# One Silu at the end of the channel norm, and three of w_out's weight blocks moved ahead of the last modulation parts

## The chip, the cores and the metric

The kernel runs on one core of one Trainium2 chip. Its engines are TensorE (PE, matmuls; PEld is its weight load), VectorE (DVE), ScalarE (ACT), GpSimd (POOL) and SyncE (SP, which here only issues DMAs). Each engine executes its own queue in order, and semaphores make it wait for others. The metric is the device time of one execution in microseconds, as the median of several.

## The reference

The program is a chain of three parts on 272 tokens (16 meta tokens and 256 others) of width 1024: a first block of two layers, then a mixer and an expert layer with modulation. Only the first block is touched. One layer of it computes

```
hn = rmsnorm(h);  q, k, v, u = split(hn @ w_in)
attn = diff_attention(rope(q), rope(k), v)          # 4 heads, 128-query blocks, then an rmsnorm per head
z = a * sigmoid(gate);  z = causal depthwise conv(z, width 31) + conv_b
conv = silu(layer_norm(z) * ln_g + ln_b)            # over the 512 channels: the "channel norm"
h = h + concat([attn, conv]) @ w_out                # 512 + 512 channels in, 1024 out
h = h + (silu(gate) * up) @ w_down                  # gate, up from rmsnorm(h) @ w_gate_up
```

Beside that, a modulation row for the later parts is computed from a vector c: silu(c) @ w_ada + b_ada, 6144 wide, in 24 parts of 256 columns. Nothing in the first block needs it, so its parts are spread over the two layers as filler.

## The kernel before, in words

Activations lie transposed (channels on partitions, tokens along the row). Matmuls of large weights are done in three products of halves: a weight block of 1024 x 256 is loaded into a `raw` buffer (1 MB, one DMA of SP), ACT casts it to `hi` (line 165, two instructions of four k tiles each), DVE writes the rest raw - hi to `lo` (line 166, two instructions), and PE adds hi*xh (line 172), hi*xl (173) and lo*xh (174). There are three `raw`, three `hi` and three `lo` buffers; each is used in turn and waits until its last reader is done. `weights` (line 151) does the load and the conversion and raises its priority in the scheduler.

A modulation part (`ada_parts`, line 622) loads one block of w_ada into the same `raw` ring without converting it. PE runs eight narrow matmuls on it (line 628), ACT copies the row (631), PE sums it with two matmuls of one column (633), and DVE adds the bias (634).

The end of a layer's mixing is written as a string of steps, `ORDER` (line 32), one letter each: s scores, v values, a attention, c convolution, p modulation parts, n channel norm, w one w_out weight block. A scheduler with its own timeline orders the instructions of all engines from that and from priorities; the order it finds is fixed in the program. `ADA` (line 28) says how many modulation parts each layer takes.

Attention goes by query tiles (16, 128 and 128 tokens in layer 0, the last two in layer 1; here tile 1 and tile 2 are the two of 128). For a tile: transposes of the probabilities (451) and copies (453), the products with v (459), squares with sums on ACT (463), a square root on ACT and a reciprocal on DVE (201, 202), the scaled output `osb` on DVE (468), its transposes back on PE (472), and the write of the result into `cat`, the two halves of w_out's input, by ACT (475) and DVE (476). The names in the traces are those of buffers: `biga` holds the convolution's channels, `bigb` is `cat`.

The channel norm (line 501) sums the channels with matmuls of ones (505), subtracts the mean (508, 510), sums squares (512, 513), takes root and reciprocal of the variance (201, 202), and per 128 channels multiplies (517), then builds y * sigmoid(y) from Tanh: a Tanh (519) and an Identity (520) on ACT, their product on DVE (522), the halved high part into `cat` on ACT (524) and the rest on DVE (525).

The products with w_out (lines 562 to 572) take the heads' four k tiles first for the first five output blocks, so that they can start when the attention is done and the channel norm is not. Where ACT goes over to a function of another table (Sqrt, Tanh, Exp and Silu here), the program has an ACT_TABLE_LOAD ahead of it.

Of the kernel before, what the change touches and what calls it, by code (L numbers as in the profile page):

```python
# [9 lines left out]
F32 = mybir.dt.float32  # L10
F32R = mybir.dt.float32r
I32 = mybir.dt.int32
AF = mybir.ActivationFunctionType
OP = mybir.AluOpType

NM, S, D = 16, 256, 1024
T = NM + S
# [7 lines left out]
FIRST = 2000  # L25
LAM0 = [0.8 - 0.6 * math.exp(-0.3 * l) for l in range(2)]
EARLY = 1500
ADA = (12, 10, 2)
TAPS = (((0, 31), (1, 16)), ((0, 16),))
AHEAD = 5  # L30
PR0 = 9
ORDER = ("svacpnwwww", "svacpnwwww")


GQ, GK, GV, GZ, GB, DQ, DK, DV, GA, GBB = 0, 1024, 2048, 3072, 4096, 4112, 5648, 7184, 8720, 9744
# [74 lines left out]
class K:  # L110
# [195 lines left out]
    def first_block(s):  # L306
        nc, I, V, A, PE, SP, ap, cp = s.nc, s.I, s.V, s.A, s.PE, s.SP, s.ap, s.cp
# [3 lines left out]
        with s.tc.high_priority(offset=FIRST):  # L311
# [3 lines left out]
            P = s.columns(ap, ap, (("norm1_g", 16), ("b_glu", 16)), SP, tag="scr", bufs=3)  # L315
# [11 lines left out]
        for l in range(2):  # L327
            w_in = I["w_in"][l]
            tq = NM if l else 0
            nq = T - tq  # L330
# [9 lines left out]
            def sub(t, o, a):  # L340
                return t[:, o:o + a * T].rearrange("p (a b) -> p a b", a=a)
# [3 lines left out]
            acc = sub(s1, nz, 4)  # L345
            cat = (sub(s2, 0, KC), sub(s2, KC * T, KC))
# [3 lines left out]
            for b in range(2):  # L350
# [4 lines left out]
                for j in range(2):  # L355
                    c = 2 * b + j
# [30 lines left out]
            if l == 0:  # L387
                P.update(s.columns(ap, ap, (("norm2_g", 16), ("conv_b", 8), ("conv_ln_g", 8), ("conv_ln_b", 8),
                                            ("subln_g", 2)), s.G, tag="scr", bufs=3))
                subg = ap.tile([128, 2], F32, name="subg")  # L390
                hlg = ap.tile([128, 8], F32, name="hlg")
                hlb = ap.tile([128, 8], F32, name="hlb")
                for i in range(2):
                    V.tensor_scalar(subg[:, i:i + 1], P["subln_g"][:, i:i + 1], 1.0 - LAM0[i], None, op0=OP.mult)
                V.tensor_scalar(hlg, P["conv_ln_g"], 0.5, None, op0=OP.mult)
                V.tensor_scalar(hlb, P["conv_ln_b"], 0.5, None, op0=OP.mult)
                cw, nlam = s.first_params()
                s.ada()
            rcs, pro = [], []
# [79 lines left out]
            def conv():  # L479

                for c, n in TAPS[l]:
                    p = s.dx()
                    for j in range(n):
                        dg = ap.tile([128, 128], F32, name="dg", bufs=4)
                        A.activation(dg, ident, AF.Copy, scale=cw[:, l, 4 * j + c:4 * j + c + 1])
                        PE.matmul(p[:, :nq], dg, z[:, c, tq + j:tq + j + nq], start=(j == 0), stop=(j == n - 1))  # L486
                    A.activation(acc[:, c, :nq], p[:, :nq], AF.Identity, bias=P["conv_b"][:, 4 * l + c:4 * l + c + 1])
                tp = dict(TAPS[l])
                for c0 in (0, 2):
                    for j, c in [(j, c) for j in range(CW) for c in (c0, c0 + 1)]:  # L490
                        if j < tp.get(c, 0):
                            continue
                        zz = z[:, c, tq + j:tq + j + nq]
                        wj = cw[:, l, 4 * j + c:4 * j + c + 1]
                        if j == 0:
                            V.tensor_scalar(acc[:, c, :nq], zz, wj, P["conv_b"][:, 4 * l + c:4 * l + c + 1],
                                            op0=OP.mult, op1=OP.add)
                        else:
                            V.scalar_tensor_tensor(acc[:, c, :nq], zz, wj, acc[:, c, :nq], op0=OP.mult, op1=OP.add)

            def channel_norm():

                mu = s.ax()
                for c in range(4):
                    PE.matmul(mu[:, :nq], C["ones"], acc[:, c, :nq], start=(c == 0), stop=(c == 3))
                var = s.ax()
                sd = ap.tile([128, T], F32, name="sd")
                A.activation(sd[:, :nq], mu[:, :nq], AF.Copy, scale=1.0 / 512)
                for c in range(4):
                    V.tensor_tensor(acc[:, c, :nq], acc[:, c, :nq], sd[:, :nq], op=OP.subtract)  # L510
                    sq = ap.tile([128, T], F32, name="sq", bufs=3)
                    A.activation(sq[:, :nq], acc[:, c, :nq], AF.Square)
                    PE.matmul(var[:, :nq], C["ones"], sq[:, :nq], start=(c == 0), stop=(c == 3))
                s.rsqrt(sd[:, :nq], var[:, :nq], s.eps5, 1.0 / 512)
                for c in range(4):
                    i = 4 * l + c
                    V.tensor_tensor(acc[:, c, :nq], acc[:, c, :nq], sd[:, :nq], op=OP.mult)
                    th = ap.tile([128, T], F32, name="sq", bufs=3)
                    A.activation(th[:, :nq], acc[:, c, :nq], AF.Tanh, bias=hlb[:, i:i + 1], scale=hlg[:, i:i + 1])
                    A.activation(acc[:, c, :nq], acc[:, c, :nq], AF.Identity, bias=P["conv_ln_b"][:, i:i + 1],  # L520
                                 scale=P["conv_ln_g"][:, i:i + 1])
                    V.scalar_tensor_tensor(acc[:, c, :nq], th[:, :nq], 1.0, acc[:, c, :nq], op0=OP.add, op1=OP.mult)
                    ch = cat[0][:, 4 + c, tq:]
                    A.activation(ch, acc[:, c, :nq], AF.Copy, scale=0.5)
                    V.scalar_tensor_tensor(cat[1][:, 4 + c, tq:], acc[:, c, :nq], 0.5, ch.bitcast(F32), op0=OP.mult,
                                           op1=OP.subtract)


            v = s1[:, nz + 12 * T:nz + 12 * T + 1536].rearrange("p (a b) -> p a b", a=3)

            def values():

                for b in range(2):
                    w = s.weights(w_in, 0, 8, 1024 + 256 * b)
                    pvv = s.block2([(w, 8, 0)], x, 0, T)
                    vf = ap.tile([128, 2, T], F32, name="vf", bufs=2)
                    for j in range(2):
                        V.tensor_tensor(vf[:, j], pvv[j][:, :T], r, op=OP.mult)
                    for i, (t0, n) in enumerate(QT):
                        p = s.ax()  # L540
                        for j in range(2):
                            PE.transpose(p[:n, j * 128:(j + 1) * 128], vf[:, j, t0:t0 + n], ident)
                        A.copy(v[:n, i, 256 * b:256 * b + 256], p[:n, :256])


            wo = []
            for step in ORDER[l]:
                if step == "a":
                    attention()
                elif step == "s":  # L550
                    scores()
                elif step == "v":
                    values()
                elif step == "c":
                    conv()
                elif step == "n":
                    channel_norm()
                elif step == "w":
                    wo.append(s.weights(I["w_out"][l], 0, 8, 256 * len(wo)))
                else:  # L560
                    s.ada_parts(ADA[l])
            h1 = s.hp.tile([128, KC, T], F32, name="h", bufs=2)
            ps = [(s.mm, s.mm, s.mm, s.dx, s.dx, s.ax)[j]() for j in range(AHEAD)]
            for j in range(AHEAD):
# [29 lines left out]
            if l:  # L594
                s.mix_begin()
                wada = s.ada_ahead(ADA[2])
            for b in range(4):
                ws = [(s.weights(I["w_down"][l], k0 * 128, nk, 256 * b), nk, k0) for k0, nk in ((0, 8), (8, 8), (16, 6))]
                for j, p in enumerate(s.block2(ws, (fh, fl), tq, nq)):
                    V.tensor_tensor(h[:, 2 * b + j, tq:], p[:, :nq], h1[:, 2 * b + j, tq:], op=OP.add)  # L600
                    if l:
                        with s.tc.high_priority(offset=PRI):
                            s.mix_tile(h, h1, 2 * b + j)
        s.ada_parts(ADA[2], wada)
        s.h, s.hg = h, h1
# [1122 lines left out]
```

## Time and profile before

| | |
|---|---|
| median of 3 runs | 1663.44 us (1661.53 to 1663.89) |
| profiled execution | 1670.4 us, span 1668.6 us |
| mean granted clock of PE | 0.981 |
| busy in the span: PE, DVE, ACT | 1603.3, 862.3, 757.1 us |
| DMA, mean over the span | 233 GB/s |

Times in the trace are counted from the start of the span. A line of a timeline has start, length, engine, source line, operation, output and inputs, count, and in brackets the idle time ahead of it with what ended it. A long matmul is recorded in two pieces, so "x16" on line 628 is eight matmuls, and "x24" on line 459 is twelve. The clock in the tables of stages is the share of PE's full speed that was granted; 1.00 is 2.4 GHz and 0.50 is 1.2 GHz. The DMA share counts the time that packets took, against 16 engines, and can pass 1.

### The profile page before, as it was taken

Reading aid. Unit: us, or ns where it says so; the run is one execution under the profiler, and the core shown is the slowest. Engines: PE = TensorE matmul, PEld = TensorE weight load, DVE = VectorE, ACT = ScalarE, POOL = GpSimd, SP = SyncE. Lnnn points to the kernel's source line nnn. Section 1 sums busy time; section 2 is a strip of 40 time slices with the busy share of each in tenths; the row PEclk is TensorE's granted clock in tenths of the full one; section 3 lists DMA queues with packets and bytes.
Section 4 is the critical chain, followed back from the end, with each engine's and each line's share of the span. In section 5 each row is a group of like instructions: output and inputs, shape, how many; then the busy total and the mean of one; then the engine's idle time right before and its main releaser. Section 6 shows DMA issues by size and latency. Waiting matters only on the chain.

```text
span 1668.6 us, 32896 instructions
## 1 busy us (share of the span) xinstructions
PE 1603.3 (96%) x13616; PEld 1358.8 (81%) x13616; DVE 862.3 (52%) x1763; ACT 757.1 (45%) x1548; POOL 14.5 (1%) x28
## 2 busy tenths in 40 slices
PE   6998999999999999998999999999899999999997
PEld 6965999999967999988999899999666576556563
DVE  5685766646986666448655654554322221222122
ACT  5375644435437544455855866743322221222221
POOL 2000000000000000000000000000000000000000
PEclk9999999999988999999999999999999999999999
DMA  8408555555455555653333333556799999999995
GB/s 240 149 26 266 194 179 174 172 178 168 136 177 172 182 189 184 215 191 122 126 128 102 102 128 102 192 192 226 314 380 420 421 419 420 420 419 420 421 419 245
DMA packets 209958, 389.29 MB, mean 233 GB/s; under 512 B 8854, under 2 KB 183312, under 8 KB 184976
## 3 DMA queue, kind: packets, MB, share of 16 engines
q1 hardware_dynamic: 209104, 386.66, 63.1%
q8 instruction: 108, 1.77, 0.4%
q0 software_dynamic: 704, 0.51, 0.3%
q14 instruction: 42, 0.34, 0.1%
HBM read 386.10 MB, written 1.05 MB: 232 GB/s over the span
## 4 chain that ended last, share of the span: by engine, by line
PE 83%; DMA 7%; ACT 5%; DVE 3%; issue 1%; SPq 0%; ACTq 0%; DVEq 0%
PE mm L172 14%; PE mm L174 14%; PE mm L173 14%; PE pm L1542 9%; PE pm L1568 5%; DMA we<-in_w_exp_up 5%; PE pm L1505 3%; PE dx L486 2%; PE mm L195 1%; PE mm L196 1%; PE mm L197 1%; PE dx L628 1%; PE mm L459 1%; PE acc L1586 1%; ACT hi L165 1%; PE ax L274 1%
## 5 line engine op out<-in xcount | busy, mean ns | idle before, releaser
L166 DVE TENSOR_TENSOR lo<-raw,hi 128x1024 fp32r<-128x1024 f32 (+2 forms) x300 | 347.8, 1191 | 144.7 <-ACT hi L165 143.5
L165 ACT CAST hi<-raw 128x1024 fp32r<-128x1024 f32 (+2 forms) x300 | 292.7, 1024 | 267.6 <-PE mm L173 154.0
L172 PE MATMUL mm<-xh,hi 128*128 128x272 f32 (+1 forms) x1008 | 288.1, 288 | 0.0
L173 PE MATMUL mm<-xl,hi 128*128 128x272 f32 (+1 forms) x1008 | 287.8, 286 | 0.0
L174 PE MATMUL mm<-xh,lo 128*128 128x272 f32 (+1 forms) x1008 | 286.6, 286 | 0.0
L1542 PE MATMUL pm<-we,xT 128*32 128x256 f32 (+2 forms) x2048 | 194.2, 389 | 6.3 <-DMA we<-in_w_exp_up 5.5
L173 PEld LDWEIGHTS mm<-xl,hi 128*128 128x128 f32 x1008 | 189.7, 188 | 0.9
L174 PEld LDWEIGHTS mm<-xh,lo 128*128 128x128 f32 x1008 | 189.3, 188 | 0.5
L172 PEld LDWEIGHTS mm<-xh,hi 128*128 128x128 f32 x1008 | 188.5, 188 | 0.8
L1542 PEld LDWEIGHTS pm<-we,xT 128*32 128x32 f32 (+2 forms) x2048 | 123.1, 129 | 72.6 <-DMA we<-in_w_exp_up 7.8
L173 PE MATMUL mm<-bigb,hi 128*128 128x256 f32 (+1 forms) x512 | 148.6, 291 | 0.0
L172 PE MATMUL mm<-hh,hi 128*128 128x256 f32 x384 | 110.5, 291 | 7.3 <-ACT hh L702 4.2
L1568 PE MATMUL pm<-we,hT 128*32 128x512 f32 (+2 forms) x512 | 114.8, 599 | 0.4 <-DMA we<-in_w_exp_down 0.3
L173 PE MATMUL mm<-hl,hi 128*128 128x256 f32 x384 | 109.6, 286 | 0.7 <-DVE hl L703 0.7
L174 PE MATMUL mm<-hh,lo 128*128 128x256 f32 x384 | 108.6, 286 | 0.0
L1553 DVE SCALAR_TENSOR_TENSOR hp<-sil,cs,pm 128x256 f32<-128x256 f32 x26 | 17.6, 676 | 164.8 <-ACT sil L1551 164.8
L174 PE MATMUL mm<-biga,lo 128*128 128x272 f32 (+1 forms) x352 | 101.4, 288 | 0.0
L172 PE MATMUL mm<-biga,hi 128*128 128x272 f32 (+1 forms) x352 | 100.6, 286 | 0.0
L173 PEld LDWEIGHTS mm<-bigb,hi 128*128 128x128 f32 x512 | 97.9, 191 | 0.5
L1573 DVE TENSOR_TENSOR y<-pm,gt 128x512 f32<-128x512 f32 x52 | 35.8, 689 | 107.4 <-PE pm L1568 107.4
L195 PE MATMUL mm<-hi,hh 128*128 128x256 f32 x288 | 86.0, 299 | 2.0 <-DVE cacc L859 2.0
L1551 ACT ACTIVATE sil<-pm 128x256 f32<-128x256 f32 x26 | 10.0, 385 | 170.2 <-PE pm L1542 170.2
(544 smaller groups left out, 3102.7 us busy)
## 6 DMA issues: line engine op xcount, KB each, us to landing
we<-in_w_exp_gate SPq DMA_DIRECT2D x64, 1024.0 KB, 18.2
we<-in_w_exp_up SPq DMA_DIRECT2D x64, 1024.0 KB, 19.5
we<-in_w_exp_down SPq DMA_DIRECT2D x64, 1024.0 KB, 17.7
raw<-in_w_in SPq DMA_DIRECT2D x62, 1024.0 KB, 5.0
raw<-in_w_gate_up SPq DMA_DIRECT2D x44, 1024.0 KB, 5.0
raw<-in_w_ada SPq DMA_DIRECT2D x22, 1024.0 KB, 6.2
raw<-in_w_down SPq DMA_DIRECT2D x16, 1024.0 KB, 5.1
raw<-in_w_out SPq DMA_DIRECT2D x12, 1024.0 KB, 5.4
```

Of the source, the lines that this page charges most:

```text
L165: s.A.copy(hi[:, a:b], raw[:, a:b])
L166: s.V.tensor_tensor(lo[:, a:b], raw[:, a:b], hi[:, a:b].bitcast(F32), op=OP.subtract)
L172: s.PE.matmul(ps[:, :n], a, xh, start=start, stop=False)
L173: s.PE.matmul(ps[:, :n], a, xl, start=False, stop=False)
L174: s.PE.matmul(ps[:, :n], b, xh, start=False, stop=stop)
L195: s.PE.matmul(p[:, :256], xh, w[0][:, k], start=(k == 0), stop=False)
L486: PE.matmul(p[:, :nq], dg, z[:, c, tq + j:tq + j + nq], start=(j == 0), stop=(j == n - 1))
L1505: s.PE.matmul(p[:, 256 * kk:256 * kk + 256], s.ht[h][:, i, k + kk], oh[:, i], start=(i == 0 and h == 0), stop=(i == 1 and h == 1))
L1542: mm = PE.matmul(gu[sg, 256 * m:256 * m + 256], xT[:, k, o + sg.start:o + sg.stop], w[m][:, k], start=(k == 0), stop=(k == 7))
L1553: V.scalar_tensor_tensor(hp.rearrange("p k q -> p q k"), sil.rearrange("p (q k) -> p q k", k=2), cs, gu[:, 256:].rearrange("p (q k) -> p q ...
L1568: PE.matmul(py[sg], hT[:, k, sg], w[2][:, k, 512 * j:512 * j + 512], start=(k == 0), stop=(k == 1))
L1573: V.tensor_tensor(y, py, s.gt2[:, 512 * j:512 * j + 512], op=OP.mult)
```

## The change

Two edits. The channel norm's end is one Silu with scale and bias (ACT, in place), a cast to the high half and one subtraction; a Silu of one element (`st0`) is put behind the variance's square root, so that the table of Silu is loaded there. And the parts of a layer come in two groups: `ADA` becomes ((9, 3), (8, 2), 2), and the order of steps has three w_out blocks between them, then the channel norm, then the last block.

```diff
--- before.py
+++ after.py
@@ -25,11 +25,11 @@
 FIRST = 2000
 LAM0 = [0.8 - 0.6 * math.exp(-0.3 * l) for l in range(2)]
 EARLY = 1500
-ADA = (12, 10, 2)
+ADA = ((9, 3), (8, 2), 2)
 TAPS = (((0, 31), (1, 16)), ((0, 16),))
 AHEAD = 5
 PR0 = 9
-ORDER = ("svacpnwwww", "svacpnwwww")
+ORDER = ("svacpwwwpnw", "svacpwwwpnw")
 
 
 GQ, GK, GV, GZ, GB, DQ, DK, DV, GA, GBB = 0, 1024, 2048, 3072, 4096, 4112, 5648, 7184, 8720, 9744
@@ -388,12 +388,8 @@
                 P.update(s.columns(ap, ap, (("norm2_g", 16), ("conv_b", 8), ("conv_ln_g", 8), ("conv_ln_b", 8),
                                             ("subln_g", 2)), s.G, tag="scr", bufs=3))
                 subg = ap.tile([128, 2], F32, name="subg")
-                hlg = ap.tile([128, 8], F32, name="hlg")
-                hlb = ap.tile([128, 8], F32, name="hlb")
                 for i in range(2):
                     V.tensor_scalar(subg[:, i:i + 1], P["subln_g"][:, i:i + 1], 1.0 - LAM0[i], None, op0=OP.mult)
-                V.tensor_scalar(hlg, P["conv_ln_g"], 0.5, None, op0=OP.mult)
-                V.tensor_scalar(hlb, P["conv_ln_b"], 0.5, None, op0=OP.mult)
                 cw, nlam = s.first_params()
                 s.ada()
             rcs, pro = [], []
@@ -505,6 +501,7 @@
                     PE.matmul(mu[:, :nq], C["ones"], acc[:, c, :nq], start=(c == 0), stop=(c == 3))
                 var = s.ax()
                 sd = ap.tile([128, T], F32, name="sd")
+                st0 = ap.tile([128, 1], F32, name="st0")
                 A.activation(sd[:, :nq], mu[:, :nq], AF.Copy, scale=1.0 / 512)
                 for c in range(4):
                     V.tensor_tensor(acc[:, c, :nq], acc[:, c, :nq], sd[:, :nq], op=OP.subtract)
@@ -512,19 +509,15 @@
                     A.activation(sq[:, :nq], acc[:, c, :nq], AF.Square)
                     PE.matmul(var[:, :nq], C["ones"], sq[:, :nq], start=(c == 0), stop=(c == 3))
                 s.rsqrt(sd[:, :nq], var[:, :nq], s.eps5, 1.0 / 512)
+                with s.tc.issue_after(s.last_on(A)):
+                    A.activation(st0, s.eps5, AF.Silu)
                 for c in range(4):
                     i = 4 * l + c
                     V.tensor_tensor(acc[:, c, :nq], acc[:, c, :nq], sd[:, :nq], op=OP.mult)
-                    th = ap.tile([128, T], F32, name="sq", bufs=3)
-                    A.activation(th[:, :nq], acc[:, c, :nq], AF.Tanh, bias=hlb[:, i:i + 1], scale=hlg[:, i:i + 1])
-                    A.activation(acc[:, c, :nq], acc[:, c, :nq], AF.Identity, bias=P["conv_ln_b"][:, i:i + 1],
-                                 scale=P["conv_ln_g"][:, i:i + 1])
-                    V.scalar_tensor_tensor(acc[:, c, :nq], th[:, :nq], 1.0, acc[:, c, :nq], op0=OP.add, op1=OP.mult)
-                    ch = cat[0][:, 4 + c, tq:]
-                    A.activation(ch, acc[:, c, :nq], AF.Copy, scale=0.5)
-                    V.scalar_tensor_tensor(cat[1][:, 4 + c, tq:], acc[:, c, :nq], 0.5, ch.bitcast(F32), op0=OP.mult,
-                                           op1=OP.subtract)
-
+                    a, ch = acc[:, c, :nq], cat[0][:, 4 + c, tq:]
+                    A.activation(a, a, AF.Silu, bias=P["conv_ln_b"][:, i:i + 1], scale=P["conv_ln_g"][:, i:i + 1])
+                    A.copy(ch, a)
+                    V.tensor_tensor(cat[1][:, 4 + c, tq:], a, ch.bitcast(F32), op=OP.subtract)
 
             v = s1[:, nz + 12 * T:nz + 12 * T + 1536].rearrange("p (a b) -> p a b", a=3)
 
@@ -558,7 +551,7 @@
                 elif step == "w":
                     wo.append(s.weights(I["w_out"][l], 0, 8, 256 * len(wo)))
                 else:
-                    s.ada_parts(ADA[l])
+                    s.ada_parts(ADA[l][len(wo) > 0])
             h1 = s.hp.tile([128, KC, T], F32, name="h", bufs=2)
             ps = [(s.mm, s.mm, s.mm, s.dx, s.dx, s.ax)[j]() for j in range(AHEAD)]
             for j in range(AHEAD):
```

What the scheduler makes of it is shown at four queues. Lines of the changed kernel are four to eight lower than those before from 395 on (472 is 468, 468 is 464, 628 is 621).

SP in layer 0, the loads, before:

```order
L1139 DMA rb<-in_router_bias 128x64
L158 DMA raw<-in_w_in 128x8x256 x7
L158 DMA raw<-in_w_ada 128x8x256 x12
L158 DMA raw<-in_w_out 128x8x256 x4
L158 DMA raw<-in_w_gate_up 128x8x256 x22
L158 DMA raw<-in_w_down 128x8x256 x2
```

and now:

```order
L158 DMA raw<-in_w_in 128x8x256 x7
L158 DMA raw<-in_w_ada 128x8x256 x9
L158 DMA raw<-in_w_out 128x8x256 x3
L158 DMA raw<-in_w_ada 128x8x256 x3
L158 DMA raw<-in_w_out 128x8x256
L158 DMA raw<-in_w_gate_up 128x8x256 x22
```

Three loads of w_out stand between the ninth and the tenth of w_ada; the fourth follows the twelfth.

PE in layer 0, up to the first products with w_out (172 to 174), from the last matmuls of part 9 on, before:

```order
L628 MATMUL dx<-raw,cs 32x256 x5
L513 MATMUL ax<-sq,blob_73 128x272 x3
L628 MATMUL dx<-raw,cs 32x256 x8
L633 MATMUL dx<-sel,adarow 128x1 x2
L472 MATMUL mm<-blob_73,osb 128x128 x4
L633 MATMUL dx<-sel,adarow 128x1 x2
L628 MATMUL dx<-raw,cs 32x256 x16
L633 MATMUL dx<-sel,adarow 128x1 x4
L172 MATMUL mm<-bigb,hi 128x272
```

and now:

```order
L621 MATMUL dx<-raw,cs 32x256 x5
L510 MATMUL ax<-sq,blob_73 128x272 x3
L626 MATMUL dx<-sel,adarow 128x1 x2
L621 MATMUL dx<-raw,cs 32x256 x8
L626 MATMUL dx<-sel,adarow 128x1 x2
L621 MATMUL dx<-raw,cs 32x256 x8
L468 MATMUL mm<-blob_73,osb 128x128 x4
L621 MATMUL dx<-raw,cs 32x256 x8
L626 MATMUL dx<-sel,adarow 128x1 x2
L172 MATMUL mm<-bigb,hi 128x272 x2
```

In both the matmuls of the twelfth part stand ahead of the first product; tile 2's transposes of osb have moved behind those of the tenth and eleventh part.

DVE in layer 1 up to osb of tile 1 and a little behind, before:

```order
L499 SCALAR_TENSOR_TENSOR biga<-biga,cw 128x256
L202 RECIPROCAL oss<-oss 128x4
L634 TENSOR_TENSOR mod<-dx,pc_b_ada_791 128x2
L429 SCALAR_TENSOR_TENSOR pr_4792<-pr_4793,st,pr_4792 128x272
L769 SCALAR_TENSOR_TENSOR gf<-mod,pc_b_ada_791 128x8
L499 SCALAR_TENSOR_TENSOR biga<-biga,cw 128x256
L466 TENSOR_TENSOR oss<-oss,st 128x4
L499 SCALAR_TENSOR_TENSOR biga<-biga,cw 128x256
L468 TENSOR_TENSOR osb<-mm,oss 128x512
L499 SCALAR_TENSOR_TENSOR biga<-biga,cw 128x256
L634 TENSOR_TENSOR mod<-dx,pc_b_ada_791 128x2
L166 TENSOR_TENSOR lo<-raw,hi 128x1024 x2
```

and now (two more lo halves stand above these rows):

```order
L762 SCALAR_TENSOR_TENSOR gf<-mod,pc_b_ada_787 128x8
L425 SCALAR_TENSOR_TENSOR pr_4778<-pr_4779,st,pr_4778 128x272
L166 TENSOR_TENSOR lo<-raw,hi 128x1024
L495 SCALAR_TENSOR_TENSOR biga<-biga,cw 128x256
L166 TENSOR_TENSOR lo<-raw,hi 128x1024
L202 RECIPROCAL oss<-oss 128x4
L166 TENSOR_TENSOR lo<-raw,hi 128x1024
L495 SCALAR_TENSOR_TENSOR biga<-biga,cw 128x256
L166 TENSOR_TENSOR lo<-raw,hi 128x1024
L462 TENSOR_TENSOR oss<-oss,st 128x4
L495 SCALAR_TENSOR_TENSOR biga<-biga,cw 128x256
L464 TENSOR_TENSOR osb<-mm,oss 128x512
```

The six lo halves of three w_out blocks have moved from behind osb of tile 1 to ahead of it.

ACT in layer 1, from the squares of the channel norm to its end, before:

```order
L512 ACTIVATE sq<-biga 128x256 x3
L463 ACTIVATE scr,oss<-mm,st 128x128 x3
L512 ACTIVATE sq<-biga 128x256
L463 ACTIVATE scr,oss<-mm,st 128x128
L201 ACTIVATE oss<-oss,eps_75 128x4
L201 ACTIVATE sd<-ax,eps_75 128x256
L475 ACTIVATE bigb<-mm,subg 128x4x128
L519 ACT_TABLE_LOAD
L519 ACTIVATE sq<-biga,hlb,hlg 128x256 x2
L520 ACTIVATE biga<-biga,pc_norm_g 128x256
```

and now:

```order
L201 ACTIVATE sd<-ax,eps_75 128x256
L513 ACT_TABLE_LOAD
L513 ACTIVATE st_5383<-eps_75 128x1
L459 ACTIVATE scr,oss<-mm,st 128x128 x4
L201 ACT_TABLE_LOAD
L201 ACTIVATE oss<-oss,eps_75 128x4
L518 ACT_TABLE_LOAD
L518 ACTIVATE biga<-biga,pc_norm_g 128x256 x2
L519 CAST bigb<-biga 128x256
L518 ACTIVATE biga<-biga,pc_norm_g 128x256 x2
L519 CAST bigb<-biga 128x256 x3
L471 ACTIVATE bigb<-mm,subg 128x4x128
```

The write of the heads (475, now 471) stood ahead of the table of Tanh and all work behind it; now it stands behind three table loads, the Silu and the casts, and tile 2's root has a load of its own.

## Rows read from the trace of the kernel before

**Rows 1.** Table of stages, the two ends of mixing; its first line names the columns
```profile
core 0: us, PE busy (x) PEld busy (x) DVE busy (x) ACT busy (x) POOL busy (x), PEclk, DMA share, GB/s
145.00:166.00 21.00, 16.93 (x155) 11.45 (x153) 8.57 (x23) 12.53 (x32) 0.00 (x0) 0.96 0.88 288
508.00:523.00 15.00, 13.09 (x64) 10.18 (x63) 11.60 (x17) 12.09 (x26) 0.00 (x0) 0.84 0.82 276
```

**Rows 2.** Chain of waits before layer 0's products: start us, us, what
```profile
157.39 7.62 DMA raw<-in_w_out
```

**Rows 3.** Timeline of PE, end of layer 0: start us, us, what, idle before
```profile
162.13 1.07 PE L628 MATMUL dx<-raw,cs 128*32 128x256 f32 x16 [2.24 <-DMA raw<-in_w_ada]
166.13 0.59 PE L172 MATMUL mm<-bigb,hi 128*128 128x272 f32 x1 [1.84 <-ACT hi L165]
```

**Rows 4.** Timeline of SP: issue of the last w_ada load
```profile
154.79 0.37 SPq L158 DMA_DIRECT2D raw<-in_w_ada  x1
```

**Rows 5.** Loads issued at 154.79, 142.87 and 168.50: size, us to landing
```profile
raw<-in_w_ada SPq DMA_DIRECT2D x1, 1024.0 KB, 7.2
raw<-in_w_ada SPq DMA_DIRECT2D x1, 1024.0 KB, 8.3
raw<-in_w_out SPq DMA_DIRECT2D x1, 1024.0 KB, 5.3
```

**Rows 6.** Timeline of PE, end of layer 1's mixing
```profile
501.58 1.94 PE L628 MATMUL dx<-raw,cs 128*32 128x256 f32 x16
514.15 4.29 PE L459 MATMUL mm<-biga,at 16*128 16x128 f32 x24
518.27 1.46 PE L513 MATMUL ax<-sq,blob 128*128 128x256 f32 x6
523.23 0.80 PE L172 MATMUL mm<-bigb,hi 128*128 128x256 f32 x2 [0.78 <-ACT bigb L475]
```

**Rows 7.** Timeline of DVE, end of layer 1's mixing
```profile
504.57 0.16 DVE L634 TENSOR_TENSOR mod<-dx,pc_b_ada 128x2 f32<-128x2 f32 x1 [4.18 <-PE dx L633]
507.14 0.68 DVE L468 TENSOR_TENSOR osb<-mm,oss 128x512 f32<-128x512 f32 x1
508.90 2.36 DVE L166 TENSOR_TENSOR lo<-raw,hi 128x1024 fp32r<-128x1024 f32 x2
```

**Rows 8.** Timeline of ACT, end of layer 1's mixing
```profile
503.98 1.28 ACT L201 ACT_TABLE_LOAD   x1
505.27 0.30 ACT L201 ACTIVATE oss<-oss,eps 128x4 f32<-128x4 f32 x1
520.32 0.30 ACT L201 ACTIVATE oss<-oss,eps 128x4 f32<-128x4 f32 x1
522.49 0.69 ACT L475 ACTIVATE bigb<-mm,subg 128x512 fp32r<-128x512 f32 x1 [1.29 <-PE mm L472]
523.20 1.28 ACT L519 ACT_TABLE_LOAD   x1
524.50 1.10 ACT L519 ACTIVATE sq<-biga,hlb,hlg 128x256 f32<-128x256 f32 x2
```

**Rows 9.** Groups by line: shapes, count, busy us, mean ns, idle before
```profile
L165 ACT CAST hi<-raw 128x1024 fp32r<-128x1024 f32 x276 | 275.6, 1047 | 247.2 <-PE mm L173 133.6 <-issue 105.6 <-PE mm L197 2.8
L519 ACT ACTIVATE sq<-biga,hlb,hlg 128x272 f32<-128x272 f32 (+1 forms) x8 | 4.7, 599 | 0.0
L524 ACT ACTIVATE bigb<-biga 128x272 fp32r<-128x272 f32 (+1 forms) x8 | 3.2, 413 | 0.5 <-DVE biga L522 0.5
```

**Rows 10.** Table of shorter stretches, columns as in rows 1
```profile
160.00:163.00 3.00, 0.87 (x16) 0.49 (x16) 1.28 (x4) 2.78 (x6) 0.00 (x0) 1.00 1.07 364
170.00:171.00 1.00, 1.00 (x7) 1.00 (x6) 1.00 (x2) 1.00 (x3) 0.00 (x0) 0.50 1.12 315
172.00:180.00 8.00, 8.00 (x66) 8.00 (x65) 4.84 (x10) 3.19 (x6) 0.00 (x0) 1.00 0.91 298
523.00:525.00 2.00, 1.77 (x8) 1.77 (x9) 2.00 (x6) 1.97 (x3) 0.00 (x0) 0.50 0.13 44
```


## The prediction

> **What bounds the kernel now.** I read the two stages that the diff touches, one per layer of the first block: the end of the mixing, from the last modulation parts to the first product with w_out. The table of stages comes first [rows 1]: TensorE (PE) is busy 16.93 of 21.00 us in layer 0's end and 13.09 of 15.00 us in layer 1's, so time can be lost or won there, while in the products behind layer 0's end it is busy 8.00 of 8.00 us [rows 10], so that a late start of the products is handed on whole. In layer 0 the DMA share is 0.88 over the stage. The chain of waits shows what ends last there [rows 2]: the load of w_out's first columns, 7.62 us. PE says the same with two waits, 2.24 us for the last w_ada load and 1.84 us for ScalarE's (ACT) conversion of w_out's first half [rows 3]. SP issues a load when a raw buffer is free: the last w_ada at 154.79 [rows 4], when part 9's matmuls are done, w_out's first at 157.39. So layer 0's end is a queue of loads of 1 MB. Layer 1's end is another thing: the last wait in front of its products is for ACT's write of the heads' output (bigb L475) [rows 6], and that write waited 1.29 us for PE's transposes L472 [rows 8]: the attention chain of the last query tile. Channel norm is later than that and hides behind products on the heads.
>
> **Channel norm.** Per layer four Tanh (599 ns [rows 9]), four Identity of like size and four scaled copies become four Silu and four casts; DVE loses four scalar_tensor_tensor. Before, the Tanh's load starts at 523.20 [rows 8], beside the first products, so this saving lies beside other work: 0. What counts is where the new instructions stand. In layer 0 ACT's write of the heads now comes behind the four Silu, but PE waits for a load longer than that (below): 0. In layer 1 that write comes behind a load of Silu's table that the next square root undoes, a load for the root, a second load for Silu, four Silu and four casts; before, the only load ahead of it was at 503.98, for tile 1's root [rows 8].
>
> **Layer 0.** SP's order becomes nine w_ada, three w_out, three w_ada, one w_out. The raw ring has three buffers, so w_ada 10 waits until w_out 1 is converted, 11 for 2, 12 for 3, and PE has the eight matmuls of part 12 ahead of its first product. The chain:
> - w_out 3 takes the place of the issue at 154.79. The load that stood there took 7.2 us [rows 5]: 162.0.
> - Conversion: the first hi half and two lo halves, 1047 ns [rows 9] and 2.36 us [rows 7]: 165.4. Only now is w_ada 12 issued.
> - Its load, with little beside it, as the one issued at 168.50, 5.3 us [rows 5]: 170.7.
> - Eight matmuls, 1.07 [rows 3]: the first product at 171.8 instead of 166.13, **+5.7 us**.
>
> Counted by volume it is the same: two more loads stand in front of the products, and where the queue is full it moves 364 GB/s [rows 10], 2.9 us a load: +5.8. Bounds: both loads at 5.3 us give +3.8, both at 8.3 us [rows 5] +10.6. The waits of 2.24 and 1.84 us go; the longer one for part 12's load, already in the chain, takes their place. PE's granted clock is 0.50 (1.2 GHz) in 170 to 171 after the idle times around 160 and 165, 1.00 from 172, and again 0.50 in 523 to 525 [rows 10]. PE idles more with the change, so I let both layers' products start at 1.2 GHz as they do now: 0. Bounds: a gain of 2.5 us, when layer 0's 5 us at half clock (166.13 to 171) become full ones, and a loss of as much.
>
> **Layer 1.** Three terms, from osb of tile 1 (VectorE, DVE) to the first product.
> - *DVE.* Six lo halves now stand ahead of osb. Before, DVE waits 4.18 us until 504.57 for a modulation part, and osb ends 3.25 us later, at 507.82 [rows 7]. That part's last matmuls now run ahead of the next part's eight (1.94 us [rows 6]), so DVE goes on at 502.6; then 3.25, six halves at 1.18 (2.36 for two [rows 7]), and 0.5 for small steps that change places: 513.4, +5.6.
> - *PE.* From osb to the last L459 it took 10.6 us (507.82 to 518.44 [rows 6, 7]). Now part 22's eight matmuls are inside (1.07 to 1.94; I take 1.5), and the four L513 (1.3; 1.46 for three [rows 6]). The sums L633 of parts 21 and 22 come in, while L472's wait for them before goes: 0. 513.4 + 13.4 = 526.8, +8.4.
> - *ACT.* From there to the products it took 4.8 us (518.44 to 523.23). Of these 1.9 lie between the end of tile 2's root and L475 at 522.49 [rows 8]; that stretch now holds a load (1.28), four Silu (2.0; Tanh's 1.10 for two overlap by half) and four casts (1.2, from L524's 413 ns [rows 9], overlapped): 4.5. A load for the root stands in front: 1.3. 4.8 - 1.9 + 4.5 + 1.3 = 8.7. The products start at 535.5 instead of 523.23, **+12.3 us**.
>
> Bounds: the granted clock of 0.84 over the stage [rows 1] holds 2.4 us that a full clock would give back, and a half one would take about as much more: +9.9 to +14.7. If DVE's waits hid the first two terms, the last, 3.9, would be left.
>
> A rule against this change, and a price of its own: the table load at 503.98 lasts 1.28 us, and the instruction behind it starts at 505.27 [rows 8], at once. The Trainium skill (ScalarE: Activation LUTs, Table sets: the hidden batching unit) says to finish all work of one table set before turning to another, and the same page (What ACT_TABLE_LOAD costs) puts a switch at some 2.66 us, with a drain of 1.38. By it the two extra loads of layer 1 would make the sum 20.8 instead of 18.0; the trace shows the load and no drain behind it, so I go by the row.
>
> **Sum.** 5.7 + 12.3 = 18.0 us. The profiled execution has a span of 1668.6 and 1.8 around it, 1670.4; with the change 1688.4. It is 7.0 above the median of the runs, so I carry the difference over: 1663.44 + 18.0 = **1681.4 us**. Nothing later gives it back: the w_gate_up weights wait for hi and lo buffers that these products free.
>
> **Rivals.**
> - *Layer 1 hides the conversions.* For: DVE waits 4.18 us at 504.57 [rows 7], and the loads are issued earlier. Against: DVE's order ties osb to all six halves, and the third load is issued only where the first was. ACT's 3.9 and layer 0 remain, 9.6: 1673.0.
> - *A switch costs more than its row.* An engine that empties for each load, at most a load's time again: 2 x 1.3 more, 1684.0. Against: the row behind a load [rows 8].
> - *Faster, in layer 0.* If the last w_ada loads landed early, the products would find all weights converted: the waits of 2.24 and 1.84 us go, and 2.1 us of half clock with them: 1657.3. It decides if part 12's load lands by 164. Against: by the chain it is not even issued then.
> - *No change.* The loads change places at no loss, since another wait had covered them: 1663.4. Against: the share of 0.88, and 1.07 in 160 to 163 [rows 10].
>
> **Chances.** Forecast 0.70, hidden in layer 1 0.13, dearer switches 0.05, faster 0.06, no change 0.06. The forecast's own range, from its bounds and the clock, is 1674 to 1690. With the first rival the range is 1671 to 1690; outside lie the last two and the tails of the others, some 0.18. Slower by over 0.2% (3.3 us, about what a measurement of this kernel can tell) has 0.70 + 0.13 + 0.05 = 0.88, within it 0.06, faster 0.06.
>
> **What would show it.** Layer 0: PE idle for a w_ada load right in front of its first product, near 170, and that load issued after 163. Layer 1: osb of tile 1 near 513 behind lo halves; three table loads within 15 us before the products; L475 behind four Silu. The products themselves last as long as before. The forecast is wrong if layer 0's first product with w_out starts by 167, or if layer 1's starts less than 4 us later than layer 0's shift accounts for.

## The result, and the profile after

The changed kernel takes 1683.57 us as the median of 4 runs (1679.98 to 1687.87), the kernel before 1663.66 of 4 beside it (1661.53 to 1665.96): 19.9 us slower, ratio 1.0127 (1.0113 to 1.0141). Forecast were 1681.4 us, +18.0. In a later series the same kernel took 1686.10 (5 runs) against 1662.97, ratio 1.0154 (1.0132 to 1.0176). Its profiled execution took 1685.64 us, span 1683.7.

Lines after the norm are seven lower in the changed kernel, those ahead of it four: L621 is the part's matmul (before L628), L626 its sums, L468 the heads' transposes, L471 the heads' write, L455 the products with v, L464 osb, L501 and L510 the norm's sums, L518 the Silu, L519 the cast. Its trace is already 1.4 us late at layer 0's first norm sum, where nothing is changed (L501 at 130.38, L505 before at 128.97); all shifts below are taken from that point.

**Layer 0.** TensorE ahead of the first product with w_out (start, length, what, idle ahead); this answers to [rows 3]:

```profile
164.45 1.93 PE L621 MATMUL dx<-raw,cs 128*32 128x256 f32 x16 [6.37 <-DMA raw<-in_w_ada]
...
172.81 1.93 PE L621 MATMUL dx<-raw,cs 128*32 128x256 f32 x16 [1.19 <-DMA raw<-in_w_ada]
174.68 1.01 PE L626 MATMUL dx<-sel,adarow 128*128 128x1 f32 x4
175.55 0.80 PE L172 MATMUL mm<-bigb,hi 128*128 128x272 f32 x2
```

The chain of waits through the same stretch, which answers to [rows 2] (start, us, what):

```profile
162.50 2.31 DVE lo L166 x2
164.80 0.03 DVE biga L516
164.83 7.85 DMA raw<-in_w_ada
172.68 0.14 issue
172.81 1.93 PE dx L621 x16
174.75 0.94 PE dx L626 x4
175.69 0.66 PE mm L172 x2
```

These rows hold the forecast's chain, link by link: the third converted w_out block frees the buffer for part 12's load, and part 12's eight matmuls stand in front of the first product. The first product starts at 175.55 instead of 166.13 [rows 3], 8.0 us later from the common point.

**Layer 1.** The chain again, from the first converted block to the first product:

```profile
508.06 0.14 DVE lo L166
508.20 0.92 issue
509.12 0.11 DVE gf L762
509.23 5.20 DMA raw<-in_w_ada
514.43 0.14 issue
514.56 1.94 PE dx L621 x16
516.50 2.64 PE ax L501 x8
...
527.91 1.28 ACT L513
529.19 0.01 issue
529.20 0.20 ACT st L513
529.40 1.40 ACT scr L459 x8
530.80 0.02 issue
530.82 1.28 ACT L201
532.10 0.01 issue
532.11 0.30 ACT oss L201
532.41 0.02 issue
532.43 1.28 ACT L518
533.71 0.01 issue
533.72 1.09 ACT biga L518 x2
...
537.01 0.60 ACT bigb L471
```

TensorE in that stretch, which answers to [rows 6], and osb of tile 1 on VectorE, which answers to [rows 7]:

```profile
514.56 1.94 PE L621 MATMUL dx<-raw,cs 128*32 128x256 f32 x16 [9.16 <-DMA raw<-in_w_ada]
...
519.34 0.63 PE L468 MATMUL mm<-blob,osb 128*128 128x128 f32 x4
...
527.21 1.66 PE L455 MATMUL mm<-biga,at 128*128 128x128 f32 x10
533.69 1.09 PE L468 MATMUL mm<-blob,osb 128*128 128x128 f32 x4 [4.81 <-DVE osb L464]
537.65 0.79 PE L172 MATMUL mm<-bigb,hi 128*128 128x256 f32 x2 [2.87 <-ACT bigb L471]
```

```profile
516.18 0.68 DVE L464 TENSOR_TENSOR osb<-mm,oss 128x512 f32<-128x512 f32 x1
```

Three table loads of 1.28 us (at 527.91, 530.82 and 532.43), each with the next instruction 0.01 us behind it, four Silu and four casts stand ahead of the heads' write, as forecast. New is the wait of 9.16 us on TensorE: part 21 too is loaded only when a w_out block is converted.

Against the profile of before, layer 1's first product is only 5.0 us later than layer 0's products are (13.0 at 537.65, 8.0 at layer 0's). That is not layer 1's cost: the two executions ran the stretch ahead of it at different clocks, which the second profile of before shows (below).

### The profile page after: what moved, and what is told of

It is laid out like the page before. It is cut to its first block, busy times and chain, and to the rows that moved or that the text cites. A ratio compares the mean times of both kernels' runs of the same rounds, so it can differ in the third digit from the quotient of the medians.

```text
span 1683.7 us, 32881 instructions
## 1 busy us (share of the span) xinstructions
PE 1602.5 (95%) x13616; PEld 1359.0 (81%) x13616; DVE 859.1 (51%) x1753; ACT 756.2 (45%) x1544; POOL 14.5 (1%) x28
## 4 chain that ended last, share of the span: by engine, by line
PE 81%; DMA 8%; ACT 5%; DVE 4%; issue 1%; SPq 0%; ACTq 0%; DVEq 0%
PE mm L172 14%; PE mm L173 14%; PE mm L174 14%; PE pm L1535 9%; PE pm L1561 5%; DMA we<-in_w_exp_up 5%; PE pm L1498 2%; PE dx L482 2%; DMA we<-in_w_exp_down 2%; PE mm L195 2%; PE mm L196 1%; PE mm L197 1%; PE dx L621 1%; PE ax L274 1%; PE acc L1579 1%; PE acc L1580 1%
## 5 line engine op out<-in xcount | busy, mean ns | idle before, releaser
L166 DVE TENSOR_TENSOR lo<-raw,hi 128x1024 fp32r<-128x1024 f32 (+2 forms) x300 | 348.3, 1191 | 147.5 <-ACT hi L165 146.0
```

The lines of the kernel that those rows point to most:

```text
L166: s.V.tensor_tensor(lo[:, a:b], raw[:, a:b], hi[:, a:b].bitcast(F32), op=OP.subtract)
```

## The experiments

Where the time goes is read at fixed places. The table gives how much later than in the second profile of before (e4) each profiled execution passes them, in us, after lining all up at layer 0's first norm sum: the start of layer 0's first product with w_out, the end of its last sum into h1, the start of the last group of layer 1's convolution matmuls, its first product and last sum, the start of the 32x32 products of the second block (L976 of before), and the end of the last matmul. e4 itself passes them at 164.84, 195.5, 470.2, 515.61, 543.3, 875.9 and 1652.4.

| | median, us | L0 first | L0 sum | L1 conv. | L1 first | L1 sum | block 2 | end |
|---|---|---|---|---|---|---|---|---|
| before, first profile | 1663.4 | 1.3 | 0.8 | 0.8 | 7.7 | 7.4 | 7.4 | 7.5 |
| changed | 1683.6 | 9.4 | 8.7 | 9.6 | 20.7 | 20.9 | 22.8 | 21.2 |
| changed again (e10) | 1686.1 | 9.2 | 8.4 | 9.3 | 20.4 | 20.6 | 22.6 | 21.1 |
| order only (e1) | 1700.2 | 8.3 | 8.3 | 8.3 | 19.5 | 20.4 | 32.7 | 39.5 |
| Silu only (e2) | 1663.6 | 1.2 | -0.2 | 0.7 | 9.2 | 8.9 | 8.7 | 8.8 |
| layer 0 only, three parts (e3) | 1685.5 | 7.1 | 4.4 | 5.3 | 12.0 | 10.7 | 22.6 | 24.1 |
| layer 0 only, four parts (e8) | 1670.1 | 3.8 | 4.5 | 5.4 | 6.6 | 5.3 | 5.2 | 4.6 |
| layer 1 only (e5) | 1678.4 | 0.3 | 0.3 | 1.2 | 13.1 | 13.5 | 13.7 | 14.4 |
| no early load (e6) | 1685.6 | 6.7 | 4.5 | 4.6 | 23.1 | 22.8 | 22.7 | 22.2 |
| norm behind heads (e9) | 1675.6 | 0.4 | 2.7 | 2.7 | 11.0 | 11.3 | 11.5 | 11.0 |
| four parts in gate-up (e7) | 1670.2 | 0.2 | -1.2 | 5.5 | 5.7 | 6.8 | 7.6 | 11.1 |
| old order, norm behind (e11) | 1664.1 | -0.6 | -0.9 | -0.9 | -1.2 | -2.5 | -2.5 | 0.2 |

**Order only.** The kernel before with the two tables:

```diff
-ADA = (12, 10, 2)
+ADA = ((9, 3), (8, 2), 2)
-ORDER = ("svacpnwwww", "svacpnwwww")
+ORDER = ("svacpwwwpnw", "svacpwwwpnw")
-                    s.ada_parts(ADA[l])
+                    s.ada_parts(ADA[l][len(wo) > 0])
```

> The new order of steps in both layers, the old norm with Tanh. My theory (the order is nearly all of the cost: in layer 0 the last w_ada loads stand behind three converted w_out blocks, in layer 1 six lo halves stand on VectorE in front of osb): layer 0 +8.0 us, as the changed kernel's trace has it, layer 1 about +11, in all about 1682.5. Here ScalarE's write of the heads stands behind Tanh's table load, four Tanh and the Identities, but the root and oss share one table, so one load ahead of it instead of three. Rival 1 (the cost is Silu and its table loads): within 4 us of before, 1664 to 1668. Rival 2 (all of it is layer 0's loads): also about 1682, but with layer 1's first product no later than layer 0's shift.

Measured 1700.17 (5 runs) against 1663.27, ratio 1.0221 (1.0202 to 1.0240): the sum is missed by 18 us. Layers 0 and 1 are as expected (8.3, and 11.2 from 8.3 to 19.5); the other 19 lie behind the first block, which neither edit touches: 12.3 up to the 32x32 products (see the run with layer 0 alone), and 6.8 behind them, whose cause stays open. Rival 1 falls: without any Silu the two layers cost what they cost with it. From the end of tile 2's products with v to the first product this kernel takes 8.0 us (529.10 to 537.08) with the Tanh norm and one table load, the changed kernel 8.8 with Silu and three.

**Silu only.** The changed kernel with the old `ADA`, `ORDER` and call.

> The new norm with Silu and its early table load, the old order of steps. My theory: layer 0 stays bound by loads, 0; in layer 1 the early load of the table (1.28 us) and its one-column Silu (0.20) stand in front of ScalarE's write of the heads, +1.5 us: 1665. Rival 1 (the table loads are the cost): +8 or more, 1672 to 1684. Rival 2: 1663.7. Its modulation parts around layer 1's convolution also show whether TensorE runs there at 1.2 GHz (1.93 us for eight matmul pairs, as in the profiled run of before) or 2.4 GHz (1.07, as in the changed kernel's).

Measured 1663.64 (12 runs), ratio 1.0012 (0.9995 to 1.0029). Silu and its early load, with the old order, cost nothing that can be measured, and the 1.5 us expected lie inside the interval; rival 1 falls here too. Its profiled execution had 0.50 in layer 1 from 486 to 512, like the first profile of before, so the 1.5 us ahead of the heads' write can't be told from that in the table.

**Layer 0 only.** The changed kernel with layer 1's tables as before:

```diff
-ADA = ((9, 3), (8, 2), 2)
-ORDER = ("svacpwwwpnw", "svacpwwwpnw")
+ADA = ((9, 3), (10, 0), 2)
+ORDER = ("svacpwwwpnw", "svacpnwwww")
```

> Silu in both layers, the new order in layer 0 alone. My theory: +8.0 in layer 0 and +1.5 in layer 1: 1673. Rival 1 (the table loads): as e2 or as the changed kernel, whichever holds the loads, with no difference between this kernel and the one with layer 1's order alone. Rival 2 (all of it is layer 0's loads): 1682 to 1684.

Measured 1685.51 (5 runs), ratio 1.0124 (1.0105 to 1.0143), 12 us above the expectation and like rival 2. The table shows where: 10.7 at layer 1's last sum, 22.6 in block 2. The scheduler, whose timeline the first block shifts, laid VectorE's rows of the second block's convolutions and conversions out in another order here, as it did in the run of the order alone; in the changed kernel only a few of these rows change places. ScalarE's rows of that stretch are in another order too. From where VectorE's change starts (L852 the convolutions' taps, L166 conversions; - Silu only, + this run):

```
 L852 SCALAR_TENSOR_TENSOR cacc<-mm,gcw,cacc 128x253
-L852 SCALAR_TENSOR_TENSOR cacc<-mm,gcw,cacc 128x254
-L166 TENSOR_TENSOR lo<-raw,hi 128x1024
-L852 SCALAR_TENSOR_TENSOR cacc<-mm,gcw,cacc 128x255
-L166 TENSOR_TENSOR lo<-raw,hi 128x1024
+L166 TENSOR_TENSOR lo<-raw,hi 128x1024
+L852 SCALAR_TENSOR_TENSOR cacc<-mm,gcw,cacc 128x254
+L166 TENSOR_TENSOR lo<-raw,hi 128x1024
+L852 SCALAR_TENSOR_TENSOR cacc<-mm,gcw,cacc 128x253 x2
```

The same stretch (from the transposes at L683 of before to the 32x32 products) in this run and in the next one (window, length, busy us of PE, PEld, DVE, ACT and POOL, PE's granted clock, DMA share, GB/s):

```profile
752.70:898.80 146.10, 128.88 (x1499) 123.72 (x1497) 89.94 (x182) 90.77 (x203) 1.38 (x1) 0.93 0.37 119
```

```profile
748.30:882.40 134.10, 124.03 (x1498) 119.21 (x1496) 89.94 (x182) 88.48 (x200) 1.38 (x1) 0.96 0.40 130
```

The same instructions on VectorE, 89.94 us of them, and 12.0 us more of time: TensorE waits some 7 us more, and is busy 4.9 us longer at a lower clock. No run changes this order alone; what speaks for it as the cause is that the two kernels with the new order lose 12 us here (12.3 and 11.9) and the others at most 2. So the runs e1 and e3 measure something besides the first block, and are read only up to layer 1's last sum.

**Layer 0 only, with four parts behind the weights**, whose second block is in the order of before:

```diff
-ADA = ((9, 3), (10, 0), 2)
+ADA = ((8, 4), (10, 0), 2)
```

> Layer 0's new order alone, as in the run with layer 0 alone, but with four modulation parts behind the three w_out blocks instead of three; by the order of instructions its second block is as in the kernel before, where the run with three had VectorE's rows of the second block in another order and lost 12 us there. My theory: +5 to +8 for layer 0 and 0 to +1.5 for the early load in layer 1: 1669 to 1672. Rival (layer 0's order itself costs the 22 us): 1684 to 1688.

Measured 1670.08 (12 runs), ratio 1.0042 (1.0027 to 1.0056): +6.6 us, inside my theory's range. The rival falls. On TensorE part 12's matmuls come behind the first product here.

**Layer 1 only.** `ADA = ((12, 0), (8, 2), 2)`, `ORDER = ("svacpnwwww", "svacpwwwpnw")`.

> Silu in both layers, the new order in layer 1 alone. My theory: layer 0 as before, layer 1 about +11 to +12, with osb of tile 1 behind six lo halves and three table loads in front of the heads' write: 1675. Rival 1 (the table loads; three of them stand here): 1668 from the loads alone. Rival 2 (layer 0 alone): 1664 to 1665.

Measured 1678.40 (6 runs), ratio 1.0090 (1.0070 to 1.0110): +15.1, above the 12 expected. The trace, 14.4 at its end, has 11.9 from layer 1's convolution to its first product (1.2 to 13.1), and the rest in small steps ahead and behind. Both rivals fall. The two layers apart give 6.6 + 15.1 = 21.7, together 19.9 and 23.1.

**The kernel before again**, unchanged.

> The kernel before once more, for a second profile of it. Its profiled execution was 7 us above its median, and TensorE ran at a granted clock of 0.50 in layer 1 from about 488 to 512 us. My theory: how long these half-clock stretches last differs from one execution to the next, and most of the 7 us lies there; an execution with a mean clock of 0.985 or more shows less of it, and the time from layer 1's convolution to its first product (82.2 us in the first profile) is then several us shorter. Rival: the stretch is the same in all executions, 82 us again, and layer 1's cost is the 4 us that the two first profiles show.

One run, 1663.16 us at a mean clock of 0.985, at its median where the first profile was 7 us above. From layer 1's first convolution matmul to the first product it takes 75.3 us (440.33 to 515.61) where the first took 82.2. The window from 488 to 512 in the first profile and in this one, columns as above:

```profile
488.00:512.00 24.00, 23.28 (x133) 15.22 (x126) 12.58 (x39) 12.52 (x34) 1.10 (x2) 0.52 0.78 253
```

```profile
488.00:512.00 24.00, 22.26 (x158) 16.63 (x158) 17.90 (x43) 17.66 (x46) 1.10 (x2) 0.86 1.03 327
```

At 0.52 TensorE is as busy and does fewer instructions. The theory holds, and the first profile, on which the prediction rests, was slow in just the stretch ahead of layer 1's terms. Measured from this profile layer 1 costs 11.1 us (9.6 to 20.7).

**No early load.** The changed kernel without `st0` and its Silu.

> The changed kernel without the one-column Silu that loads the table early: in layer 1 the two roots then share one table and one load stands in front of Silu instead of two, 2 x 1.28 + 0.2 us less in front of the heads' write. My theory (the write of the heads is on the path in layer 1, not in layer 0): 2.8 us less than the changed kernel, 1680.7. Rival (the lo halves on VectorE and the modulation parts alone set layer 1's end): the same as the changed kernel, 1683.6.

Measured 1685.61 (5 runs), ratio 1.0121 (1.0099 to 1.0142): no clear gain beside the changed kernel's 1.0127 and 1.0154. The 2.8 us of my theory are 0.0017 of the ratio, less than the two intervals can tell, so the medians decide neither for it nor for the rival. The segment did get shorter, from the end of tile 2's products with v (532.87) to the first product 7.1 us instead of 8.8:

```profile
531.21 1.66 PE L455 MATMUL mm<-biga,at 128*128 128x128 f32 x10
...
539.98 0.80 PE L172 MATMUL mm<-bigb,hi 128*128 128x256 f32 x2 [2.60 <-ACT bigb L471]
```

That is 1.7 of the 2.8 expected. Why nothing of it shows in the medians I can't settle: in the one profile the granted clock was 0.50 from 490 to 522, and the mean clocks of the five runs, 0.975 to 0.979, are the changed kernel's (0.972 to 0.981).

**The norm behind the heads.** The changed kernel without `st0`, and with the root behind the heads' last write on ScalarE:

```diff
-                    A.activation(ch, p3, AF.Copy, scale=subg[:, l:l + 1])
+                    s.heads = A.activation(ch, p3, AF.Copy, scale=subg[:, l:l + 1])
...
-                s.rsqrt(sd[:, :nq], var[:, :nq], s.eps5, 1.0 / 512)
+                with s.tc.issue_after(s.heads.ins):
+                    s.rsqrt(sd[:, :nq], var[:, :nq], s.eps5, 1.0 / 512)
```

> The changed kernel, with the norm's square root and so all of Silu queued on ScalarE behind the last write of the heads, and without the early load. My theory (in layer 1 three table loads, four Silu and four casts stand in front of that write): from the last L459-like sums of tile 2 to the first product 8.8 us become about 4.8, as in the kernel before; layer 0 unchanged, since there a w_ada load ends last. 4.0 us less than the changed kernel measured on the same chip (about 1679.5). Rival (ScalarE's queue does not matter; the loads and the lo halves set the end): the same as the changed kernel.

Measured 1675.59 (6 runs), ratio 1.0072 (1.0057 to 1.0087), 10.5 us below the changed kernel on the same chip where 4 were expected. In layer 1 the segment from tile 2's products with v (end 522.57) to the first product is 5.0 us, as expected (TensorE):

```profile
520.91 1.66 PE L455 MATMUL mm<-biga,at 128*128 128x128 f32 x10
525.72 1.08 PE L468 MATMUL mm<-blob,osb 128*128 128x128 f32 x4 [3.15 <-DVE osb L464]
527.58 0.80 PE L172 MATMUL mm<-bigb,hi 128*128 128x256 f32 x2 [0.78 <-ACT bigb L471]
```

Of the surplus, the trace puts most in layer 0, which I had expected unchanged: 2.7 at its last sum where the changed kernel has 8.4 and 8.7. TensorE there:

```profile
164.32 1.94 PE L619 MATMUL dx<-raw,cs 128*32 128x256 f32 x16 [1.87 <-DMA raw<-in_w_ada]
166.18 0.82 PE L172 MATMUL mm<-bigb,hi 128*128 128x272 f32 x2
...
171.00 1.07 PE L619 MATMUL dx<-raw,cs 128*32 128x256 f32 x16
...
173.45 1.07 PE L619 MATMUL dx<-raw,cs 128*32 128x256 f32 x16
```

With the heads' write early, the scheduler puts the products ahead of parts 11 and 12, whose loads then land beside them. The loads are issued in the same order as in the changed kernel and at like times (part 10's at 156.27, there at 156.66). So the first product is late in the changed kernel because two parts' matmuls stand ahead of it in TensorE's queue while their loads are under way, and because the heads' write is late (it starts at 171.66, here at 163.14); this run moves both together.

Not all of the 5.7 us between 8.4 and 2.7 is the order, though. The runs without the early load (e6) and with layer 0 alone (e3) have the changed kernel's order on TensorE here, and lose 4.5 and 4.4 us at the last sum. In them the granted clock is 1.00 from 174 us on, in the changed kernel's two profiles it is 0.50 until 178. The stretch from 160 to 178 in e6 has 0.72, as the run with the norm behind the heads has; the changed kernel's two profiles have 0.58 and 0.55:

```profile
160.00:178.00 18.00, 12.41 (x98) 8.62 (x99) 9.55 (x19) 8.14 (x15) 0.00 (x0) 0.72 1.08 348
```

At a like clock the order of the run with the norm behind the heads is worth 1.7 us at the last sum; the other 4 go with the longer time at half clock.

**The changed kernel again.**

> The changed kernel once more, on the same chip as the other two and with a second profile. 1681 to 1686. My theory: layer 1 again waits about 9 us on TensorE for part 21's load and 12 us later than before in all; layer 0 costs 4 to 9 us according to how long the granted clock stays at 0.50 from 160 us on.

Measured 1686.10 (5 runs, 1684.56 to 1693.41), just above the 1681 to 1686 expected, its trace within 0.4 us of the first at every place of the table. TensorE again waits 9.32 us for part 21's load.

**Four parts in the gate-up loop.** Silu without the early load, the old order, `ADA = (8, 10, 2)`, and in the loop over the gate-up blocks of layer 0:

```diff
+FF = (2, 4, 6, 8)
...
+                if not l and b in FF:
+                    s.ada_parts(1)
```

> Silu without the early load, the old order, and four of layer 0's twelve modulation parts taken out of the queue of loads and put into the gate-up loop, where DMA has room. My theory (layer 0's end is a queue of loads): four loads of 2.9 us less in front of w_out, at most 11.6 us, of which another wait (the conversions, the heads) takes over after some 4 to 6; each part costs TensorE about 1.4 us in the loop, 5.6: 1658 to 1664. Rival (layer 0's order does not matter, all is hidden): 1663.3 + 5.6 = 1669.

Measured 1670.16 (10 runs), ratio 1.0039 (1.0024 to 1.0053): slower than before, against my theory and near the rival's 1669. With four loads fewer in front of w_out the first product comes no earlier (0.2), since another wait takes over (TensorE, then VectorE):

```profile
164.19 1.11 PE L469 MATMUL mm<-blob,osb 128*128 128x128 f32 x4 [8.08 <-DVE osb L465]
```

```profile
160.09 1.84 DVE L203 RECIPROCAL sd<-sd 128x272 f32<-128x272 f32 x1
161.85 0.12 DVE L203 RECIPROCAL oss<-oss 128x4 f32<-128x4 f32 x1
...
163.46 0.68 DVE L465 TENSOR_TENSOR osb<-mm,oss 128x512 f32<-128x512 f32 x1
```

The heads' osb stands behind the norm's reciprocal, and the kernel loses 6.7 us between layer 0's last sum and layer 1's convolution (-1.2 to 5.5), where the others lose at most 1; that is near the 5.6 us I had put on the four parts. So fewer loads alone do not shorten layer 0's end: a second wait, nearly as long, stands behind them.

**The old order with the norm behind the heads**, which leaves of the change only its norm, at the cheapest place found:

> Silu with the norm's root behind the heads' write and the old order of steps: the norm of the change without any of its order. My theory: the same as before, 1661 to 1665, since Silu lies beside the first products and the heads' write is where it was. Rival (fewer norm instructions on ScalarE and VectorE bring time): 1658 to 1660.

Measured 1664.06 (12 runs), ratio 1.0004 (0.9989 to 1.0019): the same as before. No version here is faster than the kernel before.

## Why the prediction was right, point by point

- **Channel norm, 0 beside other work:** right with the old order (1.0012 and 1.0004). The sentence on layer 0's write of the heads, "PE waits for a load longer than that (below): 0", counted the time of ScalarE's queue and not its effect on the order: with that write ahead of the norm, layer 0 loses 2.7 us at its last sum, where the kernels with part 12 ahead of the products lose 4.4 to 8.7. The order as predicted held part 12 ahead of the products, so the forecast carried this cost without naming its cause.
- **Layer 0, +5.7:** the chain is right link by link; the sizes are off both ways. w_out 3 took 5.2 us (7.2 forecast), the conversion 3.4 (3.4), part 12's load 7.85 (5.3, taken as if little ran beside it; three w_ada loads were issued from 156.66 on), the matmuls 1.93 (1.07), and its two sums, 0.94, were left out. The first product is 8.0 later than in the first profile of before and 9.4 than in the second. As a median, layer 0 alone costs 6.6 with four parts behind the weights, within the bounds of 3.8 to 10.6; but there TensorE has part 12's matmuls behind the first product (174.45, the product at 169.94), so it is a near case and not the same one. The upper bound is a slip of the forecast: its chain with both loads at 8.3 us gives +9.8.
- **Layer 1, +12.3:** 11.1 and 11.1 in the traces of the changed kernel, 11.9 with layer 1 alone. Term by term, from the second profile of before (L459 of tile 2 ends at 510.81, its osb of tile 1 at 500.05, its first product starts at 515.61; layer 1's convolution shifts by 10.9): osb of tile 1 is 5.9 later (5.6 forecast), from osb to tile 2's products with v 12.0 us instead of 10.8 (+1.2, forecast +2.8), from there to the first product 8.8 instead of 4.8 (+4.0, forecast +3.9). The mis-sized term is PE's. The 1.3 us in it for four L513 do not follow from their row, which has 1.46 for three. And the chain does not run through osb: part 21's load held TensorE until 514.56 and L468 followed at 519.34, while osb was ready at 516.86. The lo halves ahead of osb cost nothing on top; had they been alone, they would have held L468 to within 2.5 us of it, by the same rows. So the first term's size came out on another path than the one forecast, and that part of the match is luck. No run moves part 21's load alone; its part is read from the chain. ScalarE's term is shown by a run: with the norm behind the heads' write the segment is 5.0 us again.
- **Clock, 0:** too low. In the series of the first experiments, of 17 runs of before, the five with a mean clock of 0.988 take 1660.8 to 1663.6 us and the one with 0.981 takes 1668.12; the changed kernel's first four have 0.978 to 0.981. With 0.981 one of them takes 1681.49, 13.4 more than that run of before, and 11.1 more than the first profile of before (1670.4, also 0.981). By these single runs, as an estimate, 6.5 to 9 of the 19.9 us go with a lower clock, which the longer waits of TensorE precede. In layer 0 it is 0.58 from 160 to 178 us:

```profile
160.00:178.00 18.00, 11.12 (x71) 7.00 (x72) 9.55 (x18) 8.05 (x16) 0.00 (x0) 0.58 1.03 332
```

Before had 1.00 from 172 on [rows 10]. Against the runs with the same order and 1.00 from 174 on, this costs layer 0 some 4 us (8.4 and 8.7 against 4.4 and 4.5), more than the 2.5 us that the forecast allowed.
- **The sum, 18.0 against 19.9:** the causes named are the ones found, but the closeness is partly luck. The clock of layer 0, put at 0, and layer 0's late loads add; PE's term in layer 1 was too large; and layer 1's first term was reached by another path.
- **Rivals:** layer 1 did not hide the conversions (11.1 us), the products of layer 0 start later and not earlier, which ends the faster forecast and that of no change, and a switch of tables is no dearer than its load, with 0.01 us behind each of the three. By the Trainium skill (ScalarE: Activation LUTs, What ACT_TABLE_LOAD costs) a switch would have cost 1.38 us more; the trace does not agree.

## What to carry to other kernels

A filler whose load waits for a buffer to be converted should not stand ahead of the critical matmul in an in-order queue: here TensorE stood still for 6.37 and 9.16 us at such fillers. Before a shift between two profiles is read as a cost, compare the granted clock of the stretch in both, and take a second profile where it differs. And where a scheduler lays out the whole program, compare the order of instructions to its end: two of the versions here lost 12 us in a block that their edit does not touch, and in both its order had changed.

## What was not expected of the hardware

The same program, run again, has TensorE at half clock for 24 us of layer 1 in one execution (0.52) and for much less of them in another (0.86); 6.9 of the 7.5 us between their ends arise between layer 1's convolution and its first product. Eight matmuls of a part last 1.07 us at 2.4 GHz (162.13 of before, at 1.00 [rows 3, 10]) and 1.93 at 1.2 (172.81 of the changed kernel, where the clock was 0.50).
